# Transposed probabilities move into the scores' PSUM banks, and a group's keys are prepared in a tile of their own

## The chip, the core and the metric

The kernel runs on one core of one Trainium2 chip. The metric is the device time of one execution in microseconds (us), from runs on the chip; lower is better. Engines are named as in the profile: PE is TensorE (PEld its weight load), DVE is VectorE, ACT is ScalarE, POOL is GpSimd, SP is SyncE, which here only issues DMAs.

## What is computed

One transformer layer on 512 tokens of 2048 features in fp32: sliding-window attention with sinks (32 query heads, 4 key/value heads, head width 64, window 128), then a SwiGLU block. The change lies in the attention, of which this is the core (RMS norms, rotary embedding and projections stand around it):

```
q = rms_norm(q, q_norm); k = rms_norm(k, k_norm)      # per head, then rope
scores = einsum('bnqhgd,bnkhd->bnhgqk', qb, kw) * scale    # 128 queries x 256 keys
scores = where(valid, scores, -inf)                   # band of 128
m = maximum(max(scores), sink)
p = exp(scores - m)
probs = p / (sum(p) + exp(sink - m))
out = einsum('bnhgqk,bnkhd->bnqhgd', probs, vw)
x = x + out @ w_o
```

## The kernel before

Every fp32 product is made of three products of fp32r parts: an operand is split into a high part (ACT copies it, `copy_r`, line 65) and a low part (DVE subtracts, `sub`, line 70), and PE does high x high, high x low and low x high. The weights stream in from HBM and are split so as they come: `whi` on ACT and `wlo` on DVE, twice per weight tile. PE multiplies a tile of 512 weight columns with four blocks of 128 tokens, 24 products into the four banks `acc`. These token products are written by `tok_mm` and fill most of PE's time; the program calls the stretch of 24 a tile, and measures its own time in tiles.

Attention is woven between the token products of the query projection and the first part of the output projection. PE's order is written by hand: `ev(t, fn)` puts a step at time t (in tiles), and the steps are emitted in that order. DVE and ACT are ordered by a scheduler in this part, from the order of emission, the buffers, and a priority for what stands under `soon()`. The work is cut into 32 units, eight for each of the four key/value heads (a group, `Group`): a unit is one block of 128 queries and four heads. For a unit (numbered from 0 here, n) the steps are

- `q_prep` for two units together: rope on POOL (lines 324, 326) and DVE (lines 328, 329), split into `qs` (ACT, DVE);
- `q_tr`: four transposes on PE into `ptr`, copied by ACT to `qT`;
- `soft`: eight products into `sc` (2 banks), copied by ACT and DVE (`copy_predicated`, line 482, or 484 for the first block) to `p`; then maximum, exponentials on ACT, sum, and on DVE the normalisation of `p` (line 499);
- `p_tr`: four transposes of `p` on PE into `pT`; ACT copies `ph`, DVE subtracts `pl`;
- for all but the first block of queries, POOL makes the masked copies `uh` and `ul` from them (line 516);
- `pv`: the value products into `po` (two, or four with `uh` and `ul`); ACT copies and DVE adds (lines 538, 539) into `attT`.

Before a group's first unit, `k_exp` makes `kx` (the split keys) and `k_tr` twice transposes it through a tile `ptr` into `kT0` and `kT1`.

PSUM has eight banks here: four for `acc`, two for the one tile `sc` (pool `psc`, one buffer), and two tiles of one bank each with the tag `t1` (pool `pst`), which `ptr`, `pT` and `po` take in turn. A tile can be written again when the last reader of the one before it is done. In SBUF `kx` shares the tag `qs` (two buffers) with the split queries.

When a group ends and the next begins, `stat` (squares on ACT, reduction on DVE, line 424), rope and the split of the next group's queries, and for the later groups the split of finished attention columns (`hlo`), fall together with the last units. I call these stretches the crowded ones; there are three, at units 4 to 7, 12 to 15 and 20 to 23.

Unit n starts at u = E + 2.6 + 0.98 k, with k its place in the group and E the tile at which its group's queries are complete; `q_tr` stands at u - 0.78, `soft` at u, `p_tr` at u + TT and `pv` at u + TP; `k_exp` at E - KX, the two `k_tr` at E - KA and E - KB.

Of the kernel before, what the change touches and what calls it, by code (L numbers as in the profile page):

```python
# [10 lines left out]
F32 = mybir.dt.float32  # L11
F32R = mybir.dt.float32r
# [7 lines left out]
P = 128  # L20
S = 512
D = 2048
NT = S // P
KT = D // P
HD = 64
# [21 lines left out]
def hybrid_layer(ctx, tc, x, positions, inv_freq, mixer_norm, ffn_norm, w_qkv, q_norm, k_norm, sinks,  # L47
# [15 lines left out]
    def copy_r(dst, src, scale=None):  # L63
        if scale is None:
            act.activation(dst, src, AF.Copy)  # L65
        else:
            act.activation(dst, src, AF.Copy, scale=scale)  # L67

    def sub(dst, a, b):
        dve.tensor_tensor(dst, a, b, ALU.subtract)  # L70
# [72 lines left out]
    def mm(ps, lhsT, rhs, start, stop):  # L143
        pe.matmul(ps, lhsT, rhs, start=start, stop=stop, skip_group_check=True)  # L144
# [48 lines left out]
    ap_ = attx.enter_context(tc.tile_pool(name="att", bufs=1, side="right", reuse_waits="tile"))  # L193
    psc = attx.enter_context(tc.tile_pool(name="psc", bufs=1, space=PSUM, side="right", reuse_waits="tile"))
    pst = attx.enter_context(tc.tile_pool(name="pst", bufs=2, space=PSUM, side="right", reuse_waits="tile"))
# [34 lines left out]
    def t4(ap):  # L230
        return ap.rearrange("p (t q) -> p t q", q=P)
# [171 lines left out]
    def soon():  # L403

        return tc.high_priority(offset=60)

    class Group:
# [21 lines left out]

        def k_exp(self):  # L430
            g = self.g
            kx = ap_.tile([P, 2, NT, 2, HD], F32R, tag="qs", name="kx", bufs=2)
            s4 = kc[:, :, g * HD:(g + 1) * HD].unsqueeze(2).to_broadcast([P, NT, 2, HD])
            copy_r(kx[:, 0], s4)
            sub(kx[:, 1], s4, kx[:, 0].bitcast(F32))
            self.kx = kx
# [19 lines left out]
        def q_tr(self, b, hf):  # L456
            ptr = pst.tile([P, 512], F32R, tag="t1", name="ptr")
            for h in range(4):
                pe.transpose(ptr[:, h * P:(h + 1) * P],
                             self.qs[b][:, hf * 4 + h, :, :].rearrange("p c d -> p (c d)"), identr)  # L460
            qT = ap_.tile([P, 512], F32R, tag="qT", name="qT", bufs=3)
            with soon():
                copy_r(qT, ptr.bitcast(F32))
            self.qT[b, hf] = qT

        def soft(self, b, hf):

            h0 = self.g * GRP + hf * 4
            sc = psc.tile([P, 4, 256], F32, tag="sc", name="sc")
            lo_ = 0 if b else P  # L470
            qT = self.qT.pop((b, hf))
            for h in range(4):
                q_ = qT[:, h * P:(h + 1) * P]
                ks = slice((b - 1) * P + lo_, (b + 1) * P)
                mm(sc[:, h, lo_:256], q_, self.kT[0][:, ks], True, False)
                mm(sc[:, h, lo_:256], q_, self.kT[1][:, ks], False, True)
            p_ = ap_.tile([P, 4, P], F32, tag="p", name="p", bufs=3)
            mb = mask.unsqueeze(1).to_broadcast([P, 4, P])
            with soon():
                copy_r(p_, sc[:, :, P:256])  # L480
                if b:
                    dve.copy_predicated(p_, mb, sc[:, :, 0:P])
                else:
                    dve.copy_predicated(p_, mb, negc.unsqueeze(2).to_broadcast([P, 4, P]))
            mx = ap_.tile([P, 4], F32, tag="mx", name="mx", bufs=3)
            sm = ap_.tile([P, 4], F32, tag="sm", name="sm", bufs=3)
            es = ap_.tile([P, 4], F32, tag="es", name="es", bufs=3)
            dve.tensor_reduce(mx, p_, AX.X, ALU.max)
            ff = self.f8[:, 8 * b + 4 * hf:8 * b + 4 * hf + 4]
            dve.tensor_tensor(mx, mx, ff, ALU.mult)  # L490
            dve.scalar_tensor_tensor(mx, mx, -1.0, nsink[:, h0:h0 + 4], ALU.mult, ALU.min)
            dve.tensor_tensor(es, sink_b[:, h0:h0 + 4], mx, ALU.add)
            for h in range(4):
                act.activation(p_[:, h, :], p_[:, h, :], AF.Exp, bias=mx[:, h:h + 1],
                               scale=ff[:, h:h + 1], accum_out=sm[:, h:h + 1])
            act.activation(es, es, AF.Exp)
            dve.tensor_tensor(sm, sm, es, ALU.add)
            dve.reciprocal(sm, sm)
            dve.tensor_tensor(p_, p_, sm.unsqueeze(2).to_broadcast([P, 4, P]), ALU.mult)
            self.p[b, hf] = p_  # L500

        def p_tr(self, b, hf):
            p_ = self.p.pop((b, hf))
            pT = pst.tile([P, 512], F32, tag="t1", name="pT")
            for h in range(4):
                pe.transpose(pT[:, h * P:(h + 1) * P], p_[:, h, :], ident)
            ph = ap_.tile([P, 512], F32R, tag="ph", name="ph", bufs=2)
            pl = ap_.tile([P, 512], F32R, tag="pl", name="pl", bufs=2)
            with soon():
                copy_r(ph, pT)  # L510
                sub(pl, pT, ph.bitcast(F32))
            pu = []
            if b:
                for nm, src in (("uh", ph), ("ul", pl)):
                    u = ap_.tile([P, 512], F32R, tag=nm, name=nm)
                    pool.affine_select(t4(u), t4(src.bitcast(F32)), [[0, 4], [-1, P]], ALU.is_gt, 0.0,
                                       base=0, channel_multiplier=1)
                    pu.append(u)
            self.pt[b, hf] = (ph, pl, pu)
# [19 lines left out]
                dve.tensor_tensor(attT[up, b, kt0:kt0 + 2, :], o4[up, :, 1, :], oh[up], ALU.add)  # L539

    LAG, PACE, TQ, QP = 2.6, 0.98, 0.78, 1.39
    TT, TP = 1.43, 1.99
    KX, KA, KB = 3.03, 1.98, 0.28
    for g in range(NKV):
        G = Group(g)
        E = 8 * (g + 2)
# [613 lines left out]
```

## Time and profile before

| | |
|---|---|
| median of 3 runs | 1877.67 us (1876.02 to 1879.21) |
| the profiled execution | 1879.56 us |
| its span, first to last instruction | 1877.9 us |
| PE busy | 1849.2 us, 98% |
| DVE busy | 1498.4 us, 80% |
| ACT busy | 886.7 us, 47% |
| POOL busy | 143.7 us, 8% |

An engine's busy time is what its instructions took; in a row of the timeline the first number is the start in us from the start of the span, the second how long it took, and what stands in brackets is the engine's idle time before it and what ended that. On PE and DVE neighbouring instructions overlap a little, so the distance of two starts, not the duration, is what an instruction costs in a full queue. The executions here differ from each other by up to 3.2 us.

### The profile page before, as it was taken

What the parts mean: (1) busy time and instruction counts of PE and PEld (TensorE: products, weight loads), DVE (VectorE), ACT (ScalarE), POOL (GpSimd) and SP (SyncE); (2) the same over time, 40 slices, a digit from 0 to 9 for tenths busy, and PEclk for the clock granted to TensorE, in tenths of its full rate; (3) what the DMA queues carried; (4) which work ended last, traced back from release to release, by engine and by line L of the source; (5) the groups of instructions that cost most, each with busy time, mean ns of one, the idle gap of its engine ahead of it and who ended that gap; (6) DMA issues with size and microseconds to landing.
All of it is one profiled execution on the core that took longest, in us unless ns stands there. A gap on an engine that the chain in (4) does not pass through costs nothing. (4 is left out here: it accounts for less than half of the span.)

```text
span 1877.9 us, 32549 instructions
## 1 busy us (share of the span) xinstructions
PE 1849.2 (98%) x13110; PEld 1733.3 (92%) x13110; DVE 1498.4 (80%) x2412; ACT 886.7 (47%) x1391; POOL 143.7 (8%) x182
## 2 busy tenths in 40 slices
PE   8999999999999999999999999999999999999998
PEld 6887877888889999999999999999998999999998
DVE  4568798864587888888888888888879888988887
ACT  6358888754454333333433433433435434534532
POOL 0013123010000000000000000000000111011011
PEclk9999999999999999999999999999999999999999
DMA  6321211144313433433333433333436565656665
GB/s 204 97 83 57 68 57 57 68 163 153 139 57 102 129 113 117 131 113 115 121 114 114 134 113 114 123 114 113 133 116 206 156 131 159 181 134 154 173 162 130
DMA packets 163478, 230.81 MB, mean 123 GB/s; under 512 B 10140, under 2 KB 110048, under 8 KB 162816
## 3 DMA queue, kind: packets, MB, share of 16 engines
q1 hardware_dynamic: 147712, 196.12, 32.7%
q0 software_dynamic: 15552, 32.61, 7.6%
q8 instruction: 102, 1.67, 0.4%
q14 instruction: 48, 0.39, 0.1%
q10 hardware_dynamic: 64, 0.02, 0.0%
HBM read 200.39 MB, written 31.46 MB: 123 GB/s over the span
## 5 line engine op out<-in xcount | busy, mean ns | idle before, releaser
L65 ACT ACTIVATE Whi<-W 128x1792 fp32r<-128x1792 f32 x168 | 286.5, 1705 | 518.5 <-PE acc L144 260.2
L70 DVE TENSOR_TENSOR Wlo<-W,Whi 128x1792 fp32r<-128x1792 f32 x168 | 340.3, 2026 | 128.6 <-ACT Whi L65 124.6
L144 PE MATMUL acc<-sh,Wlo 128*128 128x256 f32 x1344 | 380.4, 283 | 0.0
L144 PE MATMUL acc<-sl,Whi 128*128 128x256 f32 x1344 | 380.4, 283 | 0.0
L144 PE MATMUL acc<-sh,Whi 128*128 128x256 f32 x1344 | 380.4, 283 | 0.0
L144 PE MATMUL acc<-hhi,Wlo 128*128 128x256 f32 x1008 | 285.4, 283 | 0.5 <-DVE Wlo L70 0.5
L144 PE MATMUL acc<-hhi,Whi 128*128 128x256 f32 x1008 | 285.3, 283 | 0.0
L144 PE MATMUL acc<-hlo,Whi 128*128 128x256 f32 x1008 | 285.3, 283 | 0.0
L144 PEld LDWEIGHTS acc<-sh,Whi 128*128 128x128 f32 x1344 | 258.0, 192 | 0.0
L144 PEld LDWEIGHTS acc<-sh,Wlo 128*128 128x128 f32 x1344 | 258.0, 192 | 0.0
L144 PEld LDWEIGHTS acc<-sl,Whi 128*128 128x128 f32 x1344 | 258.0, 192 | 0.0
L144 PE MATMUL acc<-whi,hhi 128*128 128x512 f32 x512 | 207.8, 406 | 0.9 <-ACT hhi L67 0.9
L144 PE MATMUL acc<-whi,hlo 128*128 128x512 f32 x512 | 201.2, 393 | 0.0
L144 PE MATMUL acc<-wlo,hhi 128*128 128x512 f32 x512 | 200.4, 391 | 0.0
L144 PEld LDWEIGHTS acc<-hhi,Wlo 128*128 128x128 f32 x1008 | 193.5, 192 | 0.7 <-DVE Wlo L70 0.7
L144 PEld LDWEIGHTS acc<-hlo,Whi 128*128 128x128 f32 x1008 | 193.5, 192 | 0.0
L144 PEld LDWEIGHTS acc<-hhi,Whi 128*128 128x128 f32 x1008 | 193.5, 192 | 0.0
L70 DVE TENSOR_TENSOR W<-W 128x512 f32<-128x512 f32 x336 | 186.0, 553 | 9.1 <-DMA W<-ffn_w_up_in 2.5
L144 PE MATMUL acc<-dwh,sh 128*128 128x256 f32 (+1 forms) x600 | 180.4, 301 | 0.3 <-ACT row L65 0.2
L144 PE MATMUL acc<-dwh,sl 128*128 128x256 f32 (+1 forms) x600 | 180.2, 300 | 0.0
L144 PE MATMUL acc<-dwl,sh 128*128 128x256 f32 (+1 forms) x600 | 180.0, 300 | 0.0
L144 PE MATMUL acc<-dwl,hhi 128*128 128x256 f32 (+1 forms) x500 | 150.8, 302 | 1.2 <-DVE dwl L70 1.2
(286 smaller groups left out, 3574.7 us busy)
## 6 DMA issues: line engine op xcount, KB each, us to landing
W<-ffn_w_up_in SPq DMA_DIRECT2D x176, 256.0 KB, 3.0
dw<-ffn_w_down_in SPq DMA_DIRECT2D x88, 512.0 KB, 3.9
W<-ffn_w_gate_in SPq DMA_DIRECT2D x160, 256.0 KB, 3.1
wraw<-attn_w_qkv_in SPq DMA_DIRECT2D x39, 512.0 KB, 3.6
wraw<-attn_w_o_in SPq DMA_DIRECT2D x32, 512.0 KB, 3.6
actd<-U POOLq DMA_DIRECT2D x22, 512.0 KB, 3.5
raw<-actd SPq DMA_DIRECT2D x22, 512.0 KB, 4.6
x1d<-row POOLq DMA_DIRECT2D x44, 256.0 KB, 5.9
```

Source lines behind the costliest of these rows:

```text
L65: act.activation(dst, src, AF.Copy)
L70: dve.tensor_tensor(dst, a, b, ALU.subtract)
L144: pe.matmul(ps, lhsT, rhs, start=start, stop=stop, skip_group_check=True)
```

## The change

- `pT` is no longer a `t1` tile. It takes a tile with the tag `sc` from `psc`, of which there is one buffer, and uses the first of its two banks. So the scores of a unit, the transposed probabilities of the unit before, and the next scores take turns in the same tile.
- `kx` gets a tile of its own. The space comes from `qT` and `p`, which have two buffers in place of three.
- `k_exp` and the two `k_tr` are put earlier (KX 3.03 to 3.9, KA 1.98 to 2.83, KB 0.28 to 1.85 tiles before E); `pv` 0.05 tiles later.

```diff
-            kx = ap_.tile([P, 2, NT, 2, HD], F32R, tag="qs", name="kx", bufs=2)
+            kx = ap_.tile([P, 2, NT, 2, HD], F32R, tag="kx", name="kx")
...
-            qT = ap_.tile([P, 512], F32R, tag="qT", name="qT", bufs=3)
+            qT = ap_.tile([P, 512], F32R, tag="qT", name="qT", bufs=2)
...
-            p_ = ap_.tile([P, 4, P], F32, tag="p", name="p", bufs=3)
+            p_ = ap_.tile([P, 4, P], F32, tag="p", name="p", bufs=2)
...
-            pT = pst.tile([P, 512], F32, tag="t1", name="pT")
+            pT = psc.tile([P, 4, 256], F32, tag="sc", name="pT")[:, 0:2, :].rearrange("p a b -> p (a b)")
...
-    TT, TP = 1.43, 1.99
-    KX, KA, KB = 3.03, 1.98, 0.28
+    TT, TP = 1.43, 2.04
+    KX, KA, KB = 3.9, 2.83, 1.85
```

On PE, behind the value products of unit 11, the queries of unit 14 are transposed and then, in the kernel before, the second half of the next group's keys:

```order
L144 MATMUL po<-uh,d1h 128x512 [waits Pool_49]
L144 MATMUL po<-ul,d1l 128x512 [waits Pool_49]
L144 MATMUL acc_1713<-whi,hhi 128x512
L144 MATMUL acc_1713<-wlo,hhi 128x512
L144 MATMUL acc_1713<-whi,hlo 128x512
L459 MATMUL ptr<-identr,qs 128x128 [waits PE_49]
L459 MATMUL ptr<-identr,qs 128x128 x3
L441 MATMUL ptr<-identr,kx 128x128 [waits DVE_49,PE_49,Activation_49]
```

The same place in the changed kernel:

```order
L144 MATMUL po<-uh,d1h 128x512 [waits Pool_49]
L144 MATMUL po<-ul,d1l 128x512 [waits Pool_49]
L144 MATMUL acc_1713<-whi,hhi 128x512
L144 MATMUL acc_1713<-wlo,hhi 128x512
L144 MATMUL acc_1713<-whi,hlo 128x512
L459 MATMUL ptr<-identr,qs 128x128 x4
L144 MATMUL acc_1714<-whi,hhi 128x512
L144 MATMUL acc_1714<-wlo,hhi 128x512
```

The keys' transposes have gone from here; they stand two units earlier, behind the transposes of unit 10's probabilities. The same holds for the other groups.

On PE, the first score products of unit 10 in the kernel before, behind the last token products ahead of them:

```order
L144 MATMUL acc_1712<-whi,hhi 128x512
L144 MATMUL acc_1712<-wlo,hhi 128x512
L144 MATMUL acc_1712<-whi,hlo 128x512
L144 MATMUL sc<-kT_1513,qT 128x256 [waits Activation_49]
L144 MATMUL sc<-kT_1682,qT 128x256
```

And in the changed kernel:

```order
L144 MATMUL acc_1712<-whi,hhi 128x512
L144 MATMUL acc_1712<-wlo,hhi 128x512
L144 MATMUL acc_1712<-whi,hlo 128x512
L144 MATMUL sc<-kT_1415,qT 128x256 [waits DVE_49]
L144 MATMUL sc<-kT_1523,qT 128x256
```

The place is the same; the scores now wait for DVE, whose `pl` of unit 8 is the last reader of the tile.

On DVE, around `pl` of unit 12, where the second crowded stretch begins, the kernel before has

```order
L538 TENSOR_TENSOR attT<-po,oh 64x256
L539 TENSOR_TENSOR attT<-po,oh 64x256
L490 TENSOR_TENSOR mx<-mx,f_1741 128x4
L70 TENSOR_TENSOR d1h<-dv,d1h 128x64
L491 SCALAR_TENSOR_TENSOR mx<-mx,nsink 128x4
L70 TENSOR_TENSOR dv<-vc 128x64
L492 TENSOR_TENSOR es<-sink_b,mx 128x4
L424 TENSOR_REDUCE qss<-sq 128x8
L328 TENSOR_TENSOR qraw<-qraw,t1q 128x512
L329 TENSOR_TENSOR qraw<-qraw,rt 128x512
L70 TENSOR_TENSOR pl<-pT,ph 128x512
```

and the changed kernel

```order
L491 SCALAR_TENSOR_TENSOR mx<-mx,nsink 128x4
L70 TENSOR_TENSOR dv<-vc 128x64
L492 TENSOR_TENSOR es<-sink_b,mx 128x4
L70 TENSOR_TENSOR pl<-pT,ph 128x512
L497 TENSOR_TENSOR sm<-sm,es 128x4
L498 RECIPROCAL sm<-sm 128x4
L499 TENSOR_TENSOR p<-p,sm 128x512
L70 TENSOR_TENSOR wlo<-wraw,whi 128x512 x2
L424 TENSOR_REDUCE qss<-sq 128x8
L482 COPY_PREDICATED p<-mask,sc 128x512
```

One reduction (line 424) and the first rope pair (lines 328 and 329) have moved from ahead of `pl` of unit 12 to behind it; the pair stands behind the last row shown.

## Rows read from the trace of the kernel before

**Rows 1.** The page, first part: busy time of an engine, its share of the span, and its instructions.

```profile
PE 1849.2 (98%) x13110; PEld 1733.3 (92%) x13110; DVE 1498.4 (80%) x2412; ACT 886.7 (47%) x1391; POOL 143.7 (8%) x182
```

**Rows 2.** Four windows of 20 us within the attention: start and end, length, then busy time (and instructions) of PE, PEld, DVE, ACT and POOL, the granted clock of PE, the DMA share and GB/s.

```profile
160.00:180.00 20.00, 17.99 (x96) 14.50 (x96) 18.84 (x43) 17.19 (x49) 8.32 (x10) 1.00 0.17 53
180.00:200.00 20.00, 19.11 (x103) 15.79 (x102) 18.34 (x53) 14.74 (x49) 5.01 (x6) 1.00 0.21 58
240.00:260.00 20.00, 18.04 (x94) 14.38 (x93) 19.83 (x55) 16.52 (x47) 6.96 (x8) 1.00 0.16 53
320.00:340.00 20.00, 17.62 (x90) 13.96 (x90) 19.39 (x52) 15.35 (x47) 5.63 (x7) 1.00 0.16 54
```

**Rows 3.** Who PE waited for over the whole execution (the rows that touch the attention): us in total, times, longest us.

```profile
PE ptr L441 <- DVE attT L539: 3.1, 3, 1.0
PE po L144 <- DVE pl L70: 2.6, 2, 1.4
PE pT L506 <- ACT qT L65: 2.0, 3, 0.7
PE pT L506 <- DVE attT L539: 1.8, 2, 0.9
PE po L144 <- POOL ul L516: 1.4, 4, 0.4
PE pT L506 <- ACT hhi L65: 1.0, 1, 1.0
```

**Rows 4.** Timeline of PE in the second crowded stretch, the steps of attention alone: the keys' transposes, `pT` of units 12, 13 and 14, and the second value product of unit 15.

```profile
232.38 0.52 PE L441 MATMUL ptr<-identr,kx 128*128 128x128 f32 x4 [1.03 <-DVE attT L539]
234.19 0.60 PE L506 MATMUL pT<-ident,p 128*128 128x128 f32 x4
...
243.23 0.66 PE L506 MATMUL pT<-ident,p 128*128 128x128 f32 x4 [0.66 <-ACT qT L65]
...
253.24 0.63 PE L506 MATMUL pT<-ident,p 128*128 128x128 f32 x4 [0.99 <-ACT hhi L65]
...
266.37 0.50 PE L144 MATMUL po<-pl,v3l 128*128 128x512 f32 x1 [1.38 <-DVE pl L70]
```

**Rows 5.** Timeline of DVE in the same stretch: `pl` of unit 12, two neighbouring instructions, `pl` of unit 15.

```profile
235.62 0.69 DVE L70 TENSOR_TENSOR pl<-pT,ph 128x512 fp32r<-128x512 f32 x1 [0.38 <-ACT ph L65]
...
241.35 0.67 DVE L424 TENSOR_REDUCE qss<-sq 128x8 f32<-128x512 f32 x1
241.94 0.67 DVE L488 TENSOR_REDUCE mx<-p 128x4 f32<-128x512 f32 x1
...
265.63 0.69 DVE L70 TENSOR_TENSOR pl<-pT,ph 128x512 fp32r<-128x512 f32 x1
```

**Rows 6.** Timelines: the instruction of line 497 on DVE outside a crowded stretch; half a rope on POOL; then the first and the last of seven DVE instructions between `pl` of units 12 and 15 that took longer than their like elsewhere while POOL was at work (0.2 to 0.5 us each, 2.9 us together).

```profile
204.30 0.15 DVE L497 TENSOR_TENSOR sm<-sm,es 128x4 f32<-128x4 f32 x1
...
236.11 0.73 POOL L326 TENSOR_TENSOR rt<-qraw,t2q 128x256 f32<-128x256 f32 x1
...
236.23 0.63 DVE L497 TENSOR_TENSOR sm<-sm,es 128x4 f32<-128x4 f32 x1
...
263.73 0.59 DVE L490 TENSOR_TENSOR mx<-mx,f 128x4 f32<-128x4 f32 x1
```

**Rows 7.** Timelines of DVE and PE in the first and the third crowded stretch: `pl` of units 4 and 7 and the second value product of unit 7; `pl` of units 20 and 23 and the second value product of unit 23.

```profile
166.40 0.69 DVE L70 TENSOR_TENSOR pl<-pT,ph 128x512 fp32r<-128x512 f32 x1 [0.38 <-ACT ph L65]
...
194.38 0.69 DVE L70 TENSOR_TENSOR pl<-pT,ph 128x512 fp32r<-128x512 f32 x1 [0.33 <-ACT ph L65]
...
195.54 0.40 PE L144 MATMUL po<-pl,v3l 128*128 128x512 f32 x1
...
307.26 0.69 DVE L70 TENSOR_TENSOR pl<-pT,ph 128x512 fp32r<-128x512 f32 x1 [0.38 <-ACT ph L65]
...
337.00 0.69 DVE L70 TENSOR_TENSOR pl<-pT,ph 128x512 fp32r<-128x512 f32 x1
...
337.75 0.50 PE L144 MATMUL po<-pl,v3l 128*128 128x512 f32 x1 [1.17 <-DVE pl L70]
```

**Rows 8.** Timelines of PE and DVE: transposes and `pl` of a unit and the scores of the next but one, for unit 5; then `pl` and those scores for units 8, 16 and 24.

```profile
174.00 0.66 PE L506 MATMUL pT<-ident,p 128*128 128x128 f32 x4 [0.66 <-ACT qT L65]
177.40 0.69 DVE L70 TENSOR_TENSOR pl<-pT,ph 128x512 fp32r<-128x512 f32 x1
177.26 1.12 PE L144 MATMUL sc<-kT,qT 128*128 128x256 f32 x8
...
203.69 0.69 DVE L70 TENSOR_TENSOR pl<-pT,ph 128x512 fp32r<-128x512 f32 x1 [1.96 <-ACT ph L65]
204.15 1.12 PE L144 MATMUL sc<-kT,qT 128*128 128x256 f32 x8
...
275.15 0.69 DVE L70 TENSOR_TENSOR pl<-pT,ph 128x512 fp32r<-128x512 f32 x1
275.80 1.12 PE L144 MATMUL sc<-kT,qT 128*128 128x256 f32 x8
...
346.21 0.69 DVE L70 TENSOR_TENSOR pl<-pT,ph 128x512 fp32r<-128x512 f32 x1 [0.88 <-ACT ph L65]
346.71 1.12 PE L144 MATMUL sc<-kT,qT 128*128 128x256 f32 x8
```

## Prediction

> **What bounds the kernel now.** I read the page first: PE is busy 98% of the span [rows 1], so the kernel is bound by PE's own work, and a change can win only where PE stands idle, or lose by making it idle. The list of PE's waits comes next. In the attention PE waits 3.1 us for the bank of the keys' transposes, 2.0 + 1.8 + 1.0 = 4.8 us before the transposes of probabilities, and 2.6 + 1.4 = 4.0 us within the value products: 11.9 us together, 0.63% of the time [rows 3]. That is the most the change can win. The windows then show where: in the first crowded stretch PE is idle 2.01 + 0.89 = 2.90 us of 40, and in the windows of the other two about 2 us of each 20, and in the very same windows DVE is busy 18.3 to 19.8 us of 20 [rows 2]. The reader is to see these two together: PE waits just where DVE has no room. The timelines say which of the two leads. In the second stretch PE waits four times for a bank or for data, and the last wait, 1.38 us, is for `pl` of unit 15 [rows 4], which stands at the end of a DVE queue that has run without a gap since `pl` of unit 12, from 235.62 to 265.63 [rows 5]. The third stretch ends in the same wait, 1.17 us; the first does not, there `pl` of unit 7 was done 0.47 us (195.54 - 195.07) before its product started [rows 7].
>
> **The change, part by part.**
>
> Work. No engine computes more or less: the same transposes, copies and products. Only places, banks and buffers change, so everything below is waiting.
>
> The keys' transposes. Three of them waited 1.03 us each for `attT` to release a bank [rows 3, 4]. They now stand two units earlier, where `t1` serves only `ptr` and `po`, and behind them PE has had no wait. I take the 3.1 us as gone there. The keys' copy on ACT and the making of `kx` go to the same quieter place, so they cost nothing that PE sees; if that cover failed, PE would wait up to the 1.03 us again.
>
> The bank of `pT`. The transposes of probabilities no longer wait for a copy of `qT` or for `attT`: 2.0 + 1.8 us and, by its like in the other stretches, 1.0 us of the row that names `hhi` [rows 3]. But what comes after them is not free. DVE's part of the stretch must be done before `pl` of its last unit, in the order in which it is queued, and this order has changed. I count it in full-size instructions at 0.60 us, the distance of two neighbouring starts (241.35, 241.94) [rows 5].
>
> - First stretch: `pl` of units 4 and 7 start 27.98 us apart, 0.33 of it idle [rows 7]. The reduction, the first rope pair and one weight split, four instructions, now stand between them and nothing has left: 27.65 + 4 x 0.60 = 30.05 us. Its start comes earlier by the 1.03 us of the keys; ACT's copy `ph` ahead of `pl` ended the wait there, so I take 0.9 (bounds 0 and the 1.55 us of the wait and the transposes together). `pl` of unit 7 then starts at 166.40 - 0.90 + 30.05 = 195.55 and ends at 196.24. The product that needs it started at 195.54. PE comes out 0.75 us later than before.
> - Second: 30.01 us without a gap [rows 5]; three instructions enter (the reduction and the pair), three leave (the last rope pair and one `hlo`). The end moves with the start: 0.9 us earlier.
> - Third: 29.74 us [rows 7]; three enter, one rope instruction and a small one leave, + 1.13; with the start, 0.23 us later.
>
> Together + 0.75 - 0.90 + 0.23 = + 0.08 us. In words: PE's waits for banks go, and the same time comes back as waits for normalised `p`, for `pl` and for the scores' tile, because DVE's queue sets when a stretch ends. What this leans on is DVE's speed there. Seven instructions of the second stretch were held up beside POOL's work, such as a 0.15 us one that took 0.63 us, 2.9 us in all [rows 6]. POOL has the same instructions to do in the stretch, in another order, so I let six of the seven recur in each: - 0.45 x 3 = - 1.35 us. The ends are that none recurs (- 8.7) and that all do (0).
>
> The scores' tile. The scores of unit n + 2 now wait for `pl` of unit n. Between the transposes and those scores lie 12 token products, 2.60 us (174.66 to 177.26) [rows 8], or more where keys are transposed between. In the quiet stretches `pl` mostly ends well before; at the first unit of a group it doesn't: 204.38 against 204.15, 275.84 against 275.80, 346.90 against 346.71 [rows 8]. With the 0.05 us from the end of `pl` to the product that it releases [rows 4, 5], this is 0.28 + 0.09 + 0.24 = 0.6 us of new waits, with nothing behind that absorbs them. The other direction, transposes of unit n behind the copies of the scores of n + 1, is covered: the first scores of a group need ACT alone, and elsewhere the copy was done before the transposes started.
>
> A rule weighs against this part. By those rows the hand-over is covered nearly everywhere by 2.60 us of other products. The Trainium skill (Perfetto Trace Analysis, Matmuls) says that independent groups of matmuls should rotate through different PSUM banks, so that the evacuation of one overlaps the next; the change puts two groups that took turns with others into one tile. By that rule the sum would be that of the slow rival below, by the rows it is 0.6 us. No run so far shows scores and `pT` in one tile.
>
> Buffers. `qT` and `p` with two buffers: the third copy of a kind comes after the first was read on PE, in PE's own order, so nothing waits. The queries' `qs` get both their buffers for themselves; DVE and ACT read them, and PE never waited for them [rows 3]. Value products 0.05 tiles later: one or two token products change place with them. All zero.
>
> Sum: 0.08 - 1.35 + 0.6 = - 0.7 us. On the profiled execution that is 1879.56 - 0.7 = 1878.9; that execution lies 1.9 us above the median of 1877.67, so on the median 1877.0.
>
> **The rivals.** About 0.2%, 3.8 us, is what a measurement of this kernel can tell from no change.
>
> *Faster: DVE's queue does not hold.* The new order brings `pl` of units 5, 13 and 21 forward past six other instructions, and PE arrives earlier, so DVE may run with fewer hold-ups by POOL. If none recurs, the queue between the `pl`s is 2.9 us shorter in each stretch. The first stretch then ends 0.75 - 2.9 = - 2.1, the second - 3.8, the third 0.23 - 2.9 = - 2.7, and with + 0.6 the sum is - 8.0 us; with half of them - 3.7. So 1869.7 to 1874.0, say 1871.5. For it: of the PE waits many name ACT or a bank and not DVE [rows 3], and the first stretch ended without a wait for `pl` [rows 7]. Against: 19.83 of 20 us busy on DVE [rows 2].
>
> *Slower: the scores' tile stops PE and DVE in turn.* At units 5, 13 and 21 `pl` ended 178.09, the scores had started at 177.26 [rows 8]: 0.88 us of new wait with the 0.05. If that stays, DVE, whose copy of these scores is queued ahead of the normalisation of the unit before, stands still as well, and the next transposes are late by as much again: 2 x 0.88 x 3 = 5.3 us at worst, 4.0 with DVE's share at half. With all POOL hold-ups and the new waits, 0.1 + 0.6 + 4.0 = + 4.7: 1882.4. It decides from where `pl` of these units ends more than 2.60 us after its transposes. For it: 3.4 us there before. Against: the new order has this `pl` six instructions, 2 us, sooner.
>
> *Only the keys.* The bank waits come back in full elsewhere and the keys' 3.1 us stay won: - 3.1 + 0.6 = - 2.5, 1875.2. The time can't be told from the forecast; the trace can.
>
> **How the numbers follow.** Forecast, DVE's queue sets the end of the stretches (with the case of the keys alone): 0.58, with its own range 1874.5 to 1880. Faster: 0.29, since the gain rests on hold-ups that I can't place. Slower: 0.13. Of the faster rival nearly all lies beyond 0.2%, a little of the forecast too, so faster 0.30, same 0.57, slower 0.13. Leaving out about a tenth on each side, the range goes from 1870.5, near the end of the faster rival, to 1880.5.
>
> **What would show it.** Right, if the keys' transposes have no wait; if `pT` no longer waits for `qT` or `attT` but for DVE's `p`; if PE's waits in the attention still add up to 10 us or more, with the longest for `pl` of units 7, 15 and 23; if DVE has no gap between those `pl`s, and 30 us from `pl` of unit 4 to that of unit 7. The faster rival, if these spans are 28 us or less and PE waits under 8 us. The slower, if `sc` waits for `pl` by about 0.9 us at units 7, 15 and 23 and DVE then shows gaps before line 482. Wrong altogether, if time changes after the attention, where no instruction differs, or if token products wait for `wlo`.

## The result and the profile after

The changed kernel took 1882.47 us (median of 6 runs, 1880.87 to 1886.57), the kernel before, beside it, 1877.01 us (6 runs, 1874.45 to 1879.21). The ratio is 1.0030, 95% interval 1.0020 to 1.0041: it is 0.3% slower, 5.46 us, and outside the range that was forecast. The profiled execution has a span of 1881.0 us.

What PE waited for in the whole execution, the rows that touch the attention (us in total, times, longest), to be read beside [rows 3]:

```profile
PE po L144 <- DVE pl L70: 6.0, 3, 2.3
...
PE sc L144 <- DVE pl L70: 3.0, 3, 1.0
PE pT L507 <- DVE fb L78: 3.0, 2, 1.7
...
PE po L144 <- ACT ph L65: 0.9, 1, 0.9
PE po L144 <- POOL ul L517: 0.8, 2, 0.4
```

The waits for banks are gone: no row of the keys' `ptr`, none of `pT` for `qT` or `attT`. In their place PE waits for DVE: for `pl`, in the value products and now before scores too, and for the normalised `p` (the row names `fb`, the DVE instruction that ended last before it). The sum is 13.7 us against 11.9 before: 1.8 us more, which is a third of the loss. The windows show a second part. Columns as in [rows 2]; the first two are ahead of and behind the last `pl` of the second crowded stretch, the other two of the third:

```profile
262.00:268.00 6.00, 2.71 (x10) 1.34 (x8) 5.97 (x12) 4.38 (x15) 3.85 (x4) 0.97 0.00 0
268.00:274.00 6.00, 5.71 (x17) 4.87 (x18) 5.81 (x14) 2.75 (x10) 0.23 (x1) 0.50 0.26 87
338.00:344.00 6.00, 3.41 (x12) 2.20 (x11) 5.93 (x14) 3.50 (x14) 1.73 (x2) 0.90 0.10 30
344.00:350.00 6.00, 6.00 (x22) 5.04 (x22) 4.50 (x11) 3.22 (x10) 0.00 (x0) 0.53 0.16 58
```

PE was busy for 2.71 and 3.41 us of 6, and in the 6 us behind that its granted clock was 0.50 and 0.53: the lower of its two levels, 1.2 GHz instead of 2.4. In the trace's record of the clock this lasted from 267.69 to 274.51 and from 342.78 to 349.61 us, 6.83 us each. In the kernel before the clock was 1.00 through the whole attention (its one fall ahead of the last microseconds is at 1863.98, for 3.41 us). PE's timeline shows the wait and its price:

```profile
264.32 0.51 PE L144 MATMUL po<-ph,v3h 128*128 128x512 f32 x1 [0.88 <-ACT ph L65]
267.12 0.50 PE L144 MATMUL po<-pl,v3l 128*128 128x512 f32 x1 [2.30 <-DVE pl L70]
267.46 0.43 PE L144 MATMUL po<-uh,d3h 128*128 128x512 f32 x1
268.29 0.80 PE L144 MATMUL po<-ul,d3l 128*128 128x512 f32 x1 [0.40 <-POOL ul L517]
270.16 1.81 PE L144 MATMUL sc<-kT,qT 128*128 128x128 f32 x8
```

In [rows 4] PE waited 1.38 us for `pl` at this place; now it waits 0.88 us for `ph` and 2.30 for `pl`, and the next eight score products, 1.00 us behind unit 7, took 1.81.

Each run comes with the mean granted clock of its span. The six runs of the changed kernel have 0.995 to 0.998, 0.9967 on average; the averages of the kernel before, in the groups of runs that it was timed in beside the experiments, are 0.9992 to 0.9995. Such a mean takes in every fall of the clock, also those behind the attention, such as that at 1863.98.

### The profile page after: what moved, and what is told of

It reads as the page before. It is cut to its first block, busy times and chain, and to the rows that moved or that the text cites. A ratio compares the mean times of both kernels' runs of the same rounds, so it can differ in the third digit from the quotient of the medians.

```text
span 1881.0 us, 32539 instructions
## 1 busy us (share of the span) xinstructions
PE 1852.9 (99%) x13110; PEld 1736.6 (92%) x13110; DVE 1496.3 (80%) x2412; ACT 887.1 (47%) x1391; POOL 142.5 (8%) x182
## 3 DMA queue, kind: packets, MB, share of 16 engines
q8 instruction: 102, 1.67, 0.4%
```

## The experiments

Sixteen kernels, each timed in several rounds beside the kernel before on the same chip; between groups the chips differ, so the ratios compare better than the medians. Three that failed as experiments (e3, e4, e14) are not in the table but in the text. "Keys" means the expansion and the two transpositions of a group's keys. A product "that nobody reads" is a 128x512 product into a bank that the next use overwrites.

| kernel | median us | ratio to before, 95% | mean clock of its runs |
|---|---|---|---|
| the change | 1882.47 | 1.0030 (1.0020 to 1.0041) | 0.9967 |
| e1: `pT` in the scores' tile alone | 1878.73 | 1.0001 (0.9992 to 1.0010) | 0.9998 |
| e2: the change without that | 1882.65 | 1.0023 (1.0013 to 1.0033) | 0.9974 |
| e6: the line of times alone | 1884.04 | 1.0030 (1.0019 to 1.0041) | 0.9966 |
| e7: second keys earlier alone | 1882.47 | 1.0023 (1.0013 to 1.0034) | 0.9971 |
| e15: first keys earlier alone | 1882.59 | 1.0028 (1.0017 to 1.0039) | 0.9975 |
| e8: e1 and e7 together | 1881.00 | 1.0020 (1.0009 to 1.0030) | 0.9987 |
| e16: the change, second keys put back | 1884.51 | 1.0034 (1.0024 to 1.0044) | 0.9965 |
| e9: e2 with its waits filled | 1880.07 | 1.0011 (1.0002 to 1.0020) | 0.9993 |
| e5: the change with its waits filled | 1881.71 | 1.0020 (1.0011 to 1.0029) | 0.9999 |
| e13: the same, filled less | 1881.19 | 1.0021 (1.0012 to 1.0029) | 0.9993 |
| e10: e7 with its lost wait put back | 1879.51 | 1.0007 (0.9998 to 1.0016) | 0.9994 |
| e12: the change with that wait put back | 1889.41 | 1.0064 (1.0051 to 1.0076) | 0.9953 |
| e11: before with its waits filled | 1877.80 | 1.0001 (0.9993 to 1.0010) | 0.9995 |

### Which part of the change it is

e1 is the kernel before with only this:

```
-            pT = pst.tile([P, 512], F32, tag="t1", name="pT")
+            pT = psc.tile([P, 4, 256], F32, tag="sc", name="pT")[:, 0:2, :].rearrange("p a b -> p (a b)")
```

> One part alone: the transposed probabilities in the scores' tile, everything else (keys in the queries' tag and at their old times, three buffers, value products at the old time) as before. Clock theory: the changed kernel lost because PE's waits, which the queue of DVE sets, were gathered at the end of the second and the third crowded stretch, PE stood almost idle there for some 4 us, and the granted clock then fell to half for 6.83 us, 3.4 us of loss each. Here the waits of the transposes for a bank go as well, so the waits gather in the same way: one or two drops of the clock, 1880 to 1884 us. Hand-over theory (the rival): the loss is the scores' waiting for pl of the unit before the last, 3.0 us, and what follows from it; then this kernel has all of the loss and none of the keys' gain, 1884 to 1887 us, with no need of a drop of the clock.

e2 is the changed kernel with that line put back.

> The other part alone: keys in a tile of their own and earlier, two buffers of qT and p, value products later, but the transposed probabilities in a t1 tile as before. Clock theory: the transposes keep waiting for banks along the stretch, so the wait at its end stays short, the clock holds, and the keys' 3.1 us are partly won: 1874 to 1878 us. Hand-over theory: without the shared tile no loss, the keys' gain in full: 1873 to 1875 us. The two differ here by the trace: a shorter wait at the end of the stretches and no drop of the clock is asked for by the first alone.

Both expectations missed, in opposite ways. The tile costs nothing that the medians show (1.0001), although its waits came: the first rows of PE's waits in e1 are

```profile
PE sc L144 <- DVE pl L70: 5.1, 4, 1.6
...
PE ptr L441 <- DVE attT L539: 3.0, 3, 1.0
```

5.1 us before scores, and the keys' old wait is still there. The rest of the change has most of the loss or all of it (1.0023; the intervals overlap). e6 makes it one line:

```
-    KX, KA, KB = 3.03, 1.98, 0.28
+    KX, KA, KB = 3.9, 2.83, 1.85
```

> The kernel before with one line changed: the keys' preparation and transposes earlier (KX, KA, KB of the change); keys still in the queries' tag, buffers, banks and value products as before. It alone puts DVE's instructions in the crowded stretches into the order of the changed kernel. If that order is the cause, this kernel is slow as the keys' half was: 1881 to 1884 us, with PE's waits for pl at units 7, 15 and 23 of 2 us and more. If the separate tile and the two buffers are the cause (the rival), it wins the keys' wait: 1873 to 1876 us.

Nearly a hit: 1884.04 us is just above the time named, and 1.0030 is the ratio of the whole change; PE's three waits for `pl` are 5.1 us together, the longest 1.9. The loss is in the keys, the part that the prediction had taken for a pure gain. e7 takes from that line only the second transposition (`KB` 1.85), e8 the same in e1, and e15 the rest (`KX` 3.9, `KA` 2.83, with `KB` 0.28 kept); e16 is the changed kernel with `KB` at 0.28.

> The kernel before with the second transpose of the keys alone put earlier (KB 0.28 to 1.85), which leaves DVE's crowded stretches in the old order. If the order is the cause of the loss, the keys' three waits of 1.03 us go and little comes in their place: 1874 to 1877.5 us. If earlier keys cost by themselves, 1881 us or more.

> The transposed probabilities in the scores' tile and the second transpose of the keys earlier, the rest as before: the banks as in the change, DVE's order as before. If the order is the cause, 1874 to 1878 us; if banks and earlier keys only lose together, 1881 us or more.

> The kernel before with the keys expanded and their first transposition earlier (KX 3.9, KA 2.83), the second transposition where it was (KB 0.28). VectorE's order is then that of the changed kernel (6 full-size instructions ahead of `pl` of unit 4 and 34 between those of units 4 and 7, against 8 and 30), and TensorE keeps its wait for a bank at the second keys. Theory B (VectorE's order is the larger part of the loss): about 1880 to 1882 us, VectorE idle between the `pl` of units 0 and 31 for 45 us or more, and a mean clock of 0.999. Theory A (the loss comes with the lost wait and the clock): 1877 to 1878.5 us, as the kernel before.

> The changed kernel with only the second keys' transposition put back (KB 0.28 instead of 1.85); VectorE's order stays that of the changed kernel. Theory B: 1880.5 to 1882.5 us at a clock that is back at 0.999. Theory A: 1878 to 1879 us. If the clock stays at 0.997, the wait at the second keys has no part in it.

Either half of the line alone loses about as much as the whole (1.0023 and 1.0028), so the halves do not add. e7 and e8 came out at the times of the rivals named in them, but e7 is no clean test of DVE's order: it did not leave that order as it was. In its trace rope instructions have moved to later places in each crowded stretch: in the first, one instead of two stands between `pl` of units 4 and 5, and three instead of two between those of units 6 and 7. e15 came out above theory B's time and at a lower clock than it named; e16 was above it by 2 us, and its clock did not come back. So the lost wait at the second keys is not needed for the clock to fall: e15 and e16 keep a wait there (4.1 and 4.3 us in three) and have 0.9975 and 0.9965.

### Whether the clock costs the time

e3 and e4 were to keep PE at work in the waits of units 15 and 23 (e4: of unit 15), with 10 products that nobody reads between the first and the second value product:

```
             for i, (l_, r_) in enumerate(terms):
+                if i == 0 and (b, hf) == (NT - 1, 1) and self.g in (1, 2):
+                    for _ in range(10):
+                        mm(self.fill, identr, self.kT[0], True, True)
```

> The changed kernel with ten idle products (identity times keys, 512 columns, into the unused second bank of the scores' tile, read by nobody) on PE between the first and the second value product of units 15 and 23, where PE otherwise waits for pl. Ten products are 2.2 us of work at each place, less than or about the wait there. Clock theory: PE is busy through the wait, the clock holds, and though PE does 4.3 us more work the time falls by 5 to 7 us against the changed kernel: 1875 to 1878 us. Hand-over theory: nothing is won, the extra work is hidden or costs up to 1 us: 1882 to 1884 us.

> As the kernel with idle products, but at unit 15 alone. Clock theory: one drop of the clock, at the end of the third stretch, is left, and half of the loss: 1878.5 to 1881 us. Hand-over theory: 1882 to 1884 us.

They failed as experiments: 1888.84 us (1.0055, 1.0043 to 1.0067) and 1885.23 us (1.0038, 1.0026 to 1.0050). The products went into the second bank of `pT`'s tile, and the first of them waited for `pl` itself (4.5 us in two waits in e3), so they stood behind the wait and added to it. e5, e9 and e13 put them ahead of all value products of units 7, 15 and 23, into `po`'s own bank:

```
             po = pst.tile([P, 512], F32, tag="t1", name="po")
+            for _ in range(NFILL[self.g] if (b, hf) == (NT - 1, 1) else 0):
+                mm(po, identr, self.kT[0], True, True)
```

> The changed kernel with idle products (identity times keys, 512 columns, into the value products' own bank, overwritten by the first value product) on PE ahead of the value products of units 7, 15 and 23: 7, 12 and 12 of them, 1.5, 2.6 and 2.6 us, about the wait there or less. They wait for nothing, unlike the idle products tried before, which stood behind pl themselves. If the drop of the clock behind these waits is what the changed kernel lost, the clock holds and the time falls by 4 to 7 us: 1876 to 1880 us, against 1882.5. If the waits alone are the loss, nothing is won: 1882 to 1884.

> The keys moved and the transposed probabilities left in t1, as in the run of the keys alone (median 1882.65 us, mean granted clock of its runs 0.9974; its two runs at 1.000 took 1878.7 us on average), and 8 products that nobody reads ahead of the value products of units 7, 15 and 23, where TensorE waited 2.2 to 2.4 us for `pl`. At 2.92 us for 12 in the run with 7 and 12 such products these are 1.9 us of work, less than the wait. Theory A (the loss is the fall of the granted clock to half after the gathered waits): mean granted clock of the runs 0.9995 or more, time 1878 to 1880 us. Theory B (the waits themselves and VectorE's order are the loss, the clock only goes with them): the time stays at 1881.5 to 1884 us, whatever the clock.

> The changed kernel with 4, 8 and 6 products that nobody reads (at 0.243 us each 1.0, 1.9 and 1.5 us) ahead of the value products of units 7, 15 and 23, each less than TensorE's wait there (1.57, 3.18 and 2.59 us). Theory A (the clock is most of the loss): mean clock 0.9990 or more and time 1878 to 1880 us. Theory B (VectorE's queue is most of it: in the run with the longer fill it stood still for 47.4 us between the `pl` of units 0 and 31 against 39.6 before, at full clock): time 1880.5 to 1882.5 us whatever the clock.

In all three the mean clock came back (0.9999 in e5, 0.9993 in e9 and e13), though the profiled execution of e9 still has one fall, of 3.41 us. The products lie where PE stood idle: in e13 PE still waits 0.65, 1.58 and 0.76 us for `pl` behind them. But they are not the only difference, since the scheduler also moved a few instructions of DVE and ACT; in e13 six splits `hlo` stand between `pl` of units 15 and 16, in the changed kernel four. With the keys alone the time fell from 1882.65 to 1880.07 us; in the changed kernel from 1882.47 to 1881.71 and 1881.19. So the clock seems to cost something, and by these medians it is the smaller part of the change: of 5.46 us, 3.9 remain in e13 (1881.19 against 1877.31 beside it). e9 ended a little outside theory A's numbers and 1.4 us below B's. e13 came out in theory B's range, and so did e5, between the two times named for it: by them theory A, that the clock is most of the loss, does not hold in the changed kernel.

e14 filled the waits of e7 in the same way, ahead of the transpositions of p of units 6, 14 and 22:

> The kernel before with the second keys' transposition put earlier (1882.47 us, mean clock 0.9971; VectorE's order of rotations and reductions as before), and 8, 8 and 10 products that nobody reads ahead of the transpositions of p of units 6, 14 and 22, where its TensorE waited 2.4, 2.6 and 3.4 us. Theory A: mean clock 0.9990 or more and time 1877 to 1879 us, the time of the kernel before. Theory B: 1880.5 us or more at that clock.

It failed like e3: 1886.03 us (1.0044, 1.0030 to 1.0057); the products into `pT`'s bank waited for that bank (5.1 us for `attT`, 2.2 for `qT`) and came behind the wait. What of e7's loss is clock is therefore open.

### Whether a short wait guards against a long one

e10 is e7 with the second keys' four transpositions done once more at their old place, for nobody; e12 does the same in the changed kernel:

```
+        def k_idle(self):
+            ptr = pst.tile([P, 512], F32R, tag="t1", name="pidle")
+            for b in range(NT):
+                pe.transpose(ptr[:, b * P:(b + 1) * P], self.kx[:, 1, b].rearrange("p c d -> p (c d)"), identr)
...
+        ev(E - 0.28, G.k_idle)
```

> The kernel before with the second keys' transposition put earlier (median 1882.47 us, mean granted clock 0.9971 in the run of that alone), and at its old place the four transpositions once more into a t1 bank, read by nobody, so that TensorE waits there for a bank and works there as in the kernel before, while the keys are ready earlier. Theory A (TensorE's short waits ahead of the crowded stretch, taken out, gather behind it into one that the clock falls after): the wait of some 1.0 us is back at that place, no wait before `pl` or p is over 1.5 us, and the time is 1877 to 1879 us at a mean clock of 0.999. Rival C (the earlier keys reorder the other engines, VectorE above all, and that is the loss): the time stays at 1881 to 1884 us.

> The changed kernel, and at the old place of the second keys' transposition four transpositions of it once more into a t1 bank, read by nobody. Theory A (the change's loss is a wait of TensorE that gathers behind the places where its short ones were taken out, and the clock that falls after it): mean clock of the runs back from 0.9967 to 0.999 or more and the time from 1882.5 to 1878 to 1880 us, as for the second keys alone (2.96 us less, clock 0.9971 to 0.9994). Rival C (the order of VectorE with the keys' expansion earlier is the loss, which the second keys alone don't have): the time stays at 1881 to 1884 us.

e10 came near to what theory A said: the wait of 1.0 us was back three times, the clock at 0.9994, and the time at 1879.51 us, 2.96 below e7 (on another chip), though its work is larger. But it does not test the wait alone. With the four transpositions the scheduler gave DVE the order of the kernel before again: between any two neighbouring `pl`s stand as many reductions, rope instructions and splits as there, and PE's waits are those of [rows 3] to 0.1 us:

```profile
PE pidle L450 <- DVE attT L544: 3.1, 3, 1.0
PE po L144 <- DVE pl L70: 2.5, 2, 1.4
PE pT L511 <- ACT qT L65: 2.0, 3, 0.7
```

So rival C, that DVE's order is the loss, stands as well as theory A. e12 went the other way:

```profile
PE po L144 <- DVE pl L70: 7.8, 3, 3.4
...
PE pidle L450 <- DVE attT L545: 4.3, 3, 1.4
```

The wait came back (4.3 us) and the wait for `pl` did not shrink, it grew, from 6.0 to 7.8 us; with 1889.41 us neither theory's numbers held. So the short wait protects nothing by itself: the loss was small where DVE had the order of the kernel before (e10) and large where it had one like that of the change (e12). e11 asks whether filled waits help the kernel before:

> The kernel before with 5 products that nobody reads ahead of the value products of unit 15 and 3 ahead of those of unit 23, where TensorE waits 1.38 and 1.17 us for `pl`. It tries for a time below the kernel before, whose runs are at a mean granted clock of 0.9992 to 0.9994. Theory A (idle TensorE in these places costs some executions a stretch at half clock): mean clock 0.9997 or more, time 0.5 to 1 us under before, at 1876.5 to 1877.5 us. Rival: what lowers the clock of before's runs is elsewhere (the 3.41 us at half clock at 1863.98 us of its profile), and the products cost up to the 0.24 us each by which they exceed the waits: no change of the clock, time 1877.3 to 1879 us.

They do not: 1.0001, the clock as before (0.9995 beside 0.9993). PE's waits for `pl` shrank from 2.6 to 0.6 us and the time stayed: idle products that fill a wait do not end it sooner. No version beat the kernel before.

## Why the prediction was wrong, point by point

Most of what it named came true.

- The keys' transposes have no wait any more:

```profile
148.56 0.46 PE L441 MATMUL ptr<-identr,kx 128*128 128x128 f32 x4
```

- `pT` waits for DVE's p and no longer for banks; the waits in the attention are 13.7 us (10 or more were named), the longest for `pl` of units 15 (2.30), 23 (2.16) and 7 (1.57).
- From `pl` of unit 4 to that of unit 7 it worked out 30.05 us. Measured, start to start:

```profile
165.86 0.69 DVE L70 TENSOR_TENSOR pl<-pT,ph 128x512 fp32r<-128x512 f32 x1 [1.95 <-ACT ph L65]
...
195.24 0.69 DVE L70 TENSOR_TENSOR pl<-pT,ph 128x512 fp32r<-128x512 f32 x1
```

29.38 us, against 27.98 in [rows 7]. The count came near, but one of its signs did not come true: DVE has a gap in this stretch, and the like in the third (0.84 us), ahead of a rope instruction that waits for POOL.

```profile
190.84 0.69 DVE L328 TENSOR_TENSOR qraw<-qraw,t1q 128x512 f32<-128x512 f32 x1 [0.85 <-POOL rt L326]
```

- The slow rival's first half came true at its place and nearly at its price (0.88 us): the scores of units 7, 15 and 23 wait 1.0 us each for `pl` of the unit two before.

```profile
176.08 1.21 PE L144 MATMUL sc<-kT,qT 128*128 128x256 f32 x8 [1.01 <-DVE pl L70]
```

Its second half did not: in these stretches DVE's copies of line 482 show no gap ahead of them. The mechanism that the prediction held against the change is the one that e1 finds small; the near agreement of its 1882.4 us with the result is a coincidence. The rule of the Trainium skill (Perfetto Trace Analysis, Matmuls), to rotate independent groups through PSUM banks, has the sign right, as the 5.1 us of waits in e1 show; the median of e1 shows no loss, its executions at full clock 1.5 us (below).

**The step that failed first** is the one that took the stretches from the `pl` of their first unit to that of their last, and let their start come 0.9 us sooner each time because the keys' wait is gone. What the same DVE work does outside these spans was not in the sum. e13 shows it with the clock at 1.00 throughout the attention. First the kernel before, then e13; columns as in [rows 2]. The windows go from the end of one `pl` to that of another: of units 0 to 31, then 2 to 4, 4 to 7, and 15 to 16.

```profile
134.79:400.19 265.40, 253.58 (x1352) 209.71 (x1351) 225.83 (x537) 212.16 (x615) 57.71 (x71) 1.00 0.19 62
148.94:167.09 18.15, 17.12 (x95) 14.40 (x94) 13.71 (x33) 16.13 (x50) 4.78 (x7) 1.00 0.19 59
167.09:195.07 27.98, 26.10 (x137) 21.14 (x136) 27.23 (x68) 20.53 (x57) 10.23 (x12) 1.00 0.19 58
...
266.32:275.84 9.52, 9.04 (x47) 7.30 (x48) 9.31 (x22) 7.86 (x27) 1.10 (x1) 1.00 0.17 56
```

```profile
136.01:405.47 269.46, 257.62 (x1371) 212.47 (x1370) 222.23 (x535) 211.33 (x614) 56.09 (x71) 1.00 0.20 61
150.44:167.98 17.54, 17.54 (x94) 14.69 (x93) 11.93 (x30) 15.33 (x48) 4.62 (x6) 1.00 0.21 61
167.98:197.37 29.39, 26.48 (x139) 21.38 (x137) 28.02 (x72) 21.94 (x64) 9.30 (x12) 1.00 0.19 55
...
268.48:279.67 11.19, 9.14 (x46) 7.07 (x46) 11.01 (x25) 7.94 (x27) 1.09 (x1) 1.00 0.14 48
```

Read the second row of each. Units 2 to 4 lie ahead of the crowded stretch. PE's wait is indeed gone there, and it is busy for all of the 17.54 us; but the stage is only 18.15 - 17.54 = 0.61 us shorter, not 0.9, and in it DVE, which has room (11.93 of 17.54), does 13.71 - 11.93 = 1.78 us less of its work than before. That work (a reduction and a rope pair, which the prediction had seen move) now stands where DVE has hardly any room left: the stretch is 29.39 - 27.98 = 1.41 us longer, 0.79 of it DVE's work (28.02 against 27.23) and the rest DVE's idle time, the gap ahead of the rope instruction above all. In the second stretch, where three instructions leave as three enter, a rope pair goes on behind the last `pl`. From `pl` of unit 15 to that of unit 16 DVE is busy 11.01 of 11.19 us, against 9.31 of 9.52 before: 1.67 us longer. DVE's timeline of e13 there:

```profile
267.78 0.69 DVE L70 TENSOR_TENSOR pl<-pT,ph 128x512 fp32r<-128x512 f32 x1
...
269.06 1.12 DVE L328 TENSOR_TENSOR qraw<-qraw,t1q 128x512 f32<-128x512 f32 x1
...
270.78 0.68 DVE L329 TENSOR_TENSOR qraw<-qraw,rt 128x512 f32<-128x512 f32 x1
...
272.05 0.68 DVE L499 TENSOR_TENSOR p<-p,sm 128x512 f32<-128x512 f32 x1
```

Two rope instructions stand between `pl` of unit 15 and the normalisation of unit 16's `p`; before, none did (265.63 and 268.96). The third instruction more (25 against 22) is an `hlo`, and that one came with the idle products. Counted from `pl` of unit 0, those of units 7, 15, 23 and 31 come 1.08, 0.94, 3.01 and 4.07 us later than before; 2.16 of this arise between units 15 and 18, where the prediction's sum had nothing but a wait of 0.09 us. So the whole is 269.46 - 265.40 = 4.06 us longer, with DVE busy 3.60 us less, at two instructions fewer, and idle 7.66 us more. The prediction's term for hold-ups by POOL (-1.35) was too small if anything; what DVE saves, it loses as idle time. The medians have e13 3.88 us above the kernel before.

That the keys' earlier start does this is shown by e15, which changes two numbers of one line and no tile. In its profiled execution, at full clock in the attention, the same three spans are (units 0 to 31, 2 to 4, 4 to 7)

```profile
134.40:403.30 268.90, 253.20 (x1352) 209.40 (x1351) 222.93 (x536) 212.76 (x615) 56.69 (x71) 1.00 0.20 61
148.90:166.98 18.08, 16.71 (x93) 14.07 (x92) 11.87 (x30) 15.88 (x49) 4.61 (x6) 1.00 0.21 59
166.98:196.86 29.88, 26.46 (x139) 21.39 (x137) 27.81 (x73) 20.07 (x54) 9.09 (x12) 1.00 0.19 54
```

again 30 instead of 33 DVE instructions ahead of the stretch, 1.84 us less, and a stretch that is 1.90 us longer. As e15 keeps a wait at the second keys, it is not the lost wait that moves DVE's work but the order that the scheduler gives DVE once the keys stand earlier.

**What was missing altogether** is a rival for PE's clock. The prediction knew that the waits would gather before the last `pl` of a stretch and priced them by their length. Behind two of these gathered waits PE ran at 1.2 GHz for 6.83 us. The Trainium skill (TensorE: Matmul & The Clock Gate, Part 1) states two levels of the clock, 1.2 and 2.4 GHz; the trace agrees, with a granted clock of 0.50 and 1.00. The price of the falls: from `pl` of unit 0 to that of unit 31 the changed kernel's profiled execution took

```profile
134.57:407.65 273.08, 259.24 (x1353) 214.14 (x1352) 222.29 (x535) 211.69 (x614) 56.06 (x71) 0.97 0.19 60
```

273.08 us, 3.62 more than e13 with nearly the same order and a full clock. That is one execution. It is 7.68 us more than in the kernel before, while the spans differ by 3.1: behind this window the execution before took 1477.7 us and had the fall at 1863.98, that of the change 1473.4 us without one (e11, without one, 1473.3). In the medians filling the waits gave back 1.3 us (e13) and 2.6 us with the keys alone (e9 against e2), both on other chips and with intervals that overlap.

So of the 5.46 us about 3.9 are what e13 keeps when the clock is held, which I put down to DVE's queue, and about 1.5 go with the clock. This division is an estimate. The runs of one kernel against each other give the clock more: over the six runs of the change each 0.001 of mean clock goes with 1.5 us, which for the 0.0026 between 0.9967 and 0.9993 would be 4 us.

The tile has a part too, which the medians hide. e1 at full clock has a longer attention (267.53 us between the same `pl`s, 2.13 more), and its nine runs with a mean clock of 1.000 took 1878.63 us on average, 1.5 more than the eleven such runs of the kernel before beside it (1877.15). The medians agree because the kernel before has more runs below 1.000 (12 of 23, e1 2 of 11). e2's two runs at 1.000, with the keys earlier and no shared tile, took 1878.65 us, 1.5 more as well. What stays open: how the loss divides exactly between the keys, the tile and the clock; why e12 costs 7 us; and how much of e7's loss is its moved rope instructions and how much the clock.

## What to carry to other kernels

Where two engines bind in turn, an engine's spare time in the other's stage is a store: a change that moves DVE's work out of a stage which PE fills may shorten that stage little, and the work comes back where DVE binds. Steps that are only put earlier on PE can do this through the scheduler, which orders the other engines anew. Sum each engine's work over the whole cycle of stages, with what lies ahead of and behind the crowded one, and not only the queue within it. And a wait that is put together from several short ones is priced by its length only as long as the granted clock behind it stays at 1.00; look at the clock by windows, in more than one execution, before calling moved waits free. An experiment that adds work to one engine can reorder the others too: compare their orders before reading its time.

## What the runs showed of the hardware that was not expected

In the changed kernel PE's granted clock fell to 0.50 inside the attention although PE is busy 99% of the span, both times behind some microseconds in which it had waited much (2.71 us busy of 6, 3.41 of 6). With work whose result nobody reads, 4 + 8 + 6 products of about 0.25 us each, the mean clock of the runs was 0.9993 instead of 0.9967. The kernel before waited there as well, 4.62 us busy of 6, and kept 1.00:

```profile
261.00:267.00 6.00, 4.62 (x22) 3.27 (x20) 5.97 (x13) 4.85 (x15) 1.49 (x2) 1.00 0.21 80
```

But the same activity does not give the same clock each time. e10 has the same wait of 1.38 us at this place and was just as busy, and behind it its clock was at 0.50 for 6.83 us, from 268.93:

```profile
262.54:268.54 6.00, 4.62 (x22) 3.26 (x20) 5.97 (x13) 4.84 (x15) 1.50 (x2) 1.00 0.20 76
268.54:274.54 6.00, 5.57 (x18) 4.70 (x18) 5.42 (x13) 3.00 (x12) 0.48 (x1) 0.53 0.26 87
```

Nor is the fall in every execution of one kernel: e2's runs go from 1878.3 us at a mean clock of 1.000 to 1887.3 us at 0.995. One profile does not tell whether a kernel has it.
